# A decoder trunk on one Trainium2 core: two plain feature tiles instead of four ahead of the seven-product groups

## The chip, the core and the metric

The kernel runs on one NeuronCore of a Trainium2 chip. Its engines are TensorE (PE in the profile, its weight loads PEld), VectorE (DVE), ScalarE (ACT), GpSimd (POOL) and SyncE (SP); each takes its own instructions in order and waits for others by semaphores. The metric is the device time of one execution in microseconds (us), and the time given is the median over runs.

## What is computed

One step of a two-layer decoder trunk in float32, for 512 prompt tokens and 8 sample tokens at once (520 columns). Layer 0 mixes by a short convolution, layer 1 by sliding-window attention; both then have a feed-forward part and a gated embedding. The change lies in the feed-forward part:

```python
hf = rmsnorm(h, norm_ffn_g[i])
h = h + (jax.nn.silu(hf @ ffn_w_gate[i]) * (hf @ ffn_w_up[i])) @ ffn_w_down[i]
```

D_MODEL is 1024 and FFN_HIDDEN 2816, so gate and up have 22 feature tiles of 128 each.

## The kernel before

Activations lie feature-major: 128 partitions of features by 520 tokens, eight such tiles for the model width. Float32 products are made of three passes of a rounded type: each operand is split into a high half (a cast on ScalarE) and a low half (source minus high half, on VectorE, or by ScalarE and an accumulating transfer on POOL's queue, `low` with `dma`), and high by high, high by low and low by high are summed in PSUM.

In `ffn` the 22 feature tiles of gate and up are made in two ways. The first NP = 4 tiles are plain: `dense` runs 8 x 3 x 2 = 48 matmuls of 260 columns for each of the eight tensors (gate and up of four tiles), on the operands `fx` that need no norm factor; `nf.start` and `nf.spread` run among the first two and give the factor r. Lines 549 to 553 scale, apply silu and multiply. The other 18 tiles are made in ND = 9 groups of two tiles of gate and up. `gate_up` makes such a group as a 2 by 2 block product with seven products instead of eight, in the order 1, 6, 5, 7, 2, 3, 4. A product is 24 matmuls, so a group has 168 where the plain way has 192. The seven products need:

- seven activation operands, once a layer: the generator `operands` scales h to xn1 (tag D3) and xn2 (tag DP), forms t1 to t4 (E2 to E5) and splits everything to xs 1 to 7 (D4 to D10). The low halves of xs 2, 3 and 4 come by transfer.
- seven weight operands, once a group: the generator `weights` loads four blocks a11, a12, a21, a22 (w0r to w3r in the profile, 512 KB each), splits a11 for product 1, forms s1 = a21 - a22 (line 469) and s2 = s1 - a11 (line 470) for products 5 and 6, s3 = a21 - a11 (line 475) and s4 = a12 + s2 (line 480) for 7 and 3. s1 and s3 lie in tag D3, s2 and s4 in DP, so they take over the memory of xn1 and xn2. The low halves of a12 and a22 (wlE, tags E4 and E5, after t3 and t4) come by transfer; all other halves go through a ring of five buffers, the loads through a ring of six.

Each step of a generator ends at a `yield`; `prod` calls `next(ahead)` ahead of each product, so weights run two steps ahead. The text's order gives the priority: the program's scheduler fixes each engine's order by it among the instructions that it takes to be ready, and places the waits.

In the kernel before, the seven steps of `operands` are spread over the plain tensors by the tuple of line 554, and the first two weight steps stand ahead of the last plain tensor (lines 541 to 543). The results of all tiles lie in `hid`; the down projection splits them in that order and runs behind the last group.

Of the kernel before, what the change touches and what calls it, by code (L numbers as in the profile page):

```python
# [10 lines left out]
F32 = mybir.dt.float32  # L11
# [10 lines left out]
T = S + NB  # L22
TH = T // 2
KD = D // 128
FF = 2816
MF = FF // 128
NP = 4
ND = (MF - NP) // 2
PLE = 256
KP = PLE // 128  # L30
# [27 lines left out]
def _program(nc, a, o):  # L58
# [3 lines left out]
    with tile.TileContext(nc) as tc, ExitStack() as ctx:  # L62
        cp = ctx.enter_context(tc.tile_pool(name="const", bufs=1))
# [14 lines left out]
        def temp(name, dt=F32, shape=None):  # L78
            return tp.tile(shape or [128, T], dt, tag="t", name=name)
# [11 lines left out]
        def halves(t):  # L91
            return t.rearrange("p (a c) -> p a c", a=2)


        def slot(tag, shape, dt, name):
            return ap.tile(shape, dt, tag=tag, name=name)
# [5 lines left out]
        def preload(func, after):  # L102

            t = sp.tile([128, 1], F32, tag="pre", name=f"pre{func.name}")
            A.activation(t, after[:, :1], func, scale=0.0)
# [21 lines left out]
        def xpair(i, name):  # L127
            t = slot(f"X{i}", [128, 2, T], F32R, name)
            return t[:, 0, :], t[:, 1, :]
# [14 lines left out]
        def split_to(pair, src):  # L144
            A.copy(pair[0], src)
            V.tensor_tensor(pair[1], src, pair[0].bitcast(F32), ALU.subtract)
# [6 lines left out]
        def wsplit(w, name, step=8, dst=None):  # L153

            kt = w.shape[1]
            res = []
            for k0 in range(0, kt, step):
                n = min(step, kt - k0)
                raw = wr.tile([128, 8, 128], F32, tag="raw", name=f"{name}r{k0}")
                nc.sync.dma_start(raw[:, :n], w[:, k0:k0 + n, :])  # L160
                for q0 in range(0, n, 4):
                    q = min(4, n - q0)
                    if dst is None:
                        pr = wp.tile([128, 2, 4, 128], F32R, tag="pair", name=f"{name}p{k0 + q0}")
                    else:
                        pr = dst[:, :, k0 + q0:k0 + q0 + q]
                    A.copy(pr[:, 0, :q], raw[:, q0:q0 + q])
                    V.tensor_tensor(pr[:, 1, :q], raw[:, q0:q0 + q], pr[:, 0, :q].bitcast(F32), ALU.subtract)
                    res += [(pr[:, 0, i, :], pr[:, 1, i, :]) for i in range(q)]
            return res  # L170
# [8 lines left out]
        def dense(w, xs, name, mid=None, ws=None):  # L179
            ps = ps2(name)  # L180
            ws = ws or wsplit(w, name)
            for k in range(len(ws)):
                if mid and k in mid:
                    mid[k]()
                dense_k(ps, ws, xs, k)
            return ps[:, :, :TH]
# [161 lines left out]
        for j in range(KD):  # L348
            pc = pc1 if j == 1 else dense(a["w_in"][3 * j], cx, f"pc{j}") if j else None
            px_ = dense(a["w_in"][3 * j + 1], cx, f"px{j}") if j else None  # L350
            if j == 0:
                r = nm.r
                r2 = cp.tile([128, T], F32, tag="r2", name="r2")
# [25 lines left out]
        def operands(i, nf):  # L379

            n = f"{i}"
            x1 = slot("D3", [128, 4, T], F32, f"xn1{n}")
            x2 = slot("DP", [128, 4, T], F32, f"xn2{n}")
            for k in range(KD):
                V.scalar_tensor_tensor((x1, x2)[k // 4][:, k % 4], h[k], gain((N_FFN0, N_FFN1)[i], k), nf.r,
                                       ALU.mult, ALU.mult)
                if k % 4 == 3:
                    yield  # L390
            b11, b12, b21, b22 = x1[:, :, :TH], x1[:, :, TH:], x2[:, :, :TH], x2[:, :, TH:]
            t1, t2, t3, t4 = (slot(f"E{q}", [128, 4, TH], F32, f"t{q}{n}") for q in range(2, 6))
            res = {}

            def split(p, src, tag, dma=False):
                t = slot(tag, [128, 2, 4, TH], F32R, f"xs{p}{n}")
                A.copy(t[:, 0], src)
                low(t[:, 1], src, t[:, 0], dma)
                res[p] = t

            split(1, b11, "D4")
            V.tensor_tensor(t1, b12, b11, ALU.subtract)
            V.scalar_tensor_tensor(t2, t1, -1.0, b22, ALU.mult, ALU.subtract)
            yield
            split(6, t2, "D5")
            split(5, t1, "D6")
            yield
            V.tensor_tensor(t3, b12, b22, ALU.add)
            V.tensor_tensor(t4, t2, b21, ALU.add)
            yield  # L410
            split(2, b21, "D8", True)
            split(3, b22, "D9", True)
            yield
            split(7, t3, "D7")
            split(4, t4, "D10", True)
            yield res
# [114 lines left out]
        def ffn(i, fx, nf):  # L531

            hid, w = [], {}
            ops = operands(i, nf)
            ahead = weights(i, w)
            plain = [(a[f"w_{n}"][i, m], f"{n[0]}{i}{m}") for m in range(NP) for n in ("gate", "up")]
            mid = [{MID: nf.start}, {4: nf.spread}]
            ws, ps, xs = wsplit(*plain[0]), [], None
            for j in range(2 * NP):
                wn = wsplit(*plain[j + 1]) if j + 1 < 2 * NP else None  # L540
                if wn is None:
                    for _ in range(2):
                        next(ahead)
                ps.append(dense(None, fx, plain[j][1], mid[j] if j < 2 else None, ws))
                ws = wn
                if j % 2:
                    m = j // 2
                    t, u = temp(f"tg{i}{m}"), temp(f"tu{i}{m}")
                    V.tensor_tensor(halves(t), ps[j - 1], halves(nf.r), ALU.mult)
                    A.activation(t, t, AF.Silu)  # L550
                    V.tensor_tensor(halves(u), ps[j], halves(nf.r), ALU.mult)
                    hid.append(cp.tile([128, T], F32, tag=("tabc", "tabs", "k32", "r2")[m], name=f"hid{i}{m}"))
                    V.tensor_tensor(hid[m], t, u, ALU.mult)
                for _ in range((0, 2, 1, 1, 2, 1, 0, 0)[j]):
                    xs = next(ops)
            for d in range(ND):
                if d < KD:
                    t = slot(f"X{d}", [128, 2, T], F32, f"hid{i}d{d}")
                    out = [t[:, 0], t[:, 1]]
                else:  # L560
                    out = [cp.tile([128, T], F32, tag=tag, name=f"hid{i}{tag}") for tag in ("acc", "r")]
                gate_up(i, d, xs, w, ahead, out)
                hid += out
            hid2, ws = [], []
            for j, tag in enumerate(("D3", "E0", "E1", "E2", "D4", "D5", "D6", "D7", "D8", "D9", "D10", "E3", "E4", "E5")):
                if j % 5 == 0:
                    ws += wsplit(a["w_down"][i, 0, :, j // 5 * 8:min(j // 5 * 8 + 8, MF)], f"d{i}0{j}")
                nw = 1 if tag[0] == "E" else 2
                t = slot(tag, [128, nw, 2, T], F32R, f"hid{i}{tag}")
                for q in range(nw):  # L570
                    hid2.append((t[:, q, 0, :], t[:, q, 1, :]))
                    split_to(hid2[-1], hid[len(hid2) - 1])
            hid = hid2
            dp = slot("DP", [128, KP, 2, T], F32R, f"p{i}")
            pe = [(dp[:, q, 0, :], dp[:, q, 1, :]) for q in range(KP)]
            px = [xpair(k, f"px{i}{k}") for k in range(KD)]
            nq = Norm(f"q{i}")
            for m in range(KD):
                if m == 2:
                    preload(AF.Sigmoid, h[0])  # L580
                    for q in range(KP):
                        pt = temp(f"pt{i}{q}")
                        nc.sync.dma_start(pt, a["pT"][i, :, q, :])
                        split_to(pe[q], pt)
                pd = dense(a["w_down"][i, m], hid, f"d{i}{m}", ws=ws if m == 0 else None)
                resid(m, pd, nq, ((N_PLE0, N_PLE1)[i],), (px,))
            return px, pe, nq
# [12 lines left out]
        for i in range(KD + 1):  # L600
# [4 lines left out]
            m = i - 1  # L605
# [11 lines left out]
        tabc = const("tabc", [128, T])  # L617
        tabs = const("tabs", [128, T])
# [33 lines left out]
        r = nk.r  # L652
# [416 lines left out]
def _layout(i):  # L1069
# [7 lines left out]
    g, u = _wtiles(i["ffn_w_gate"]), _wtiles(i["ffn_w_up"])  # L1077
    r["w_gate"], r["w_up"] = g[:, :NP], u[:, :NP]
    gu = np.stack([g[:, NP:], u[:, NP:]], 3).reshape(2, ND, 2, 128, 2, 2, 4, 128)
    r["w_gu"] = gu.transpose(0, 1, 2, 5, 3, 4, 6, 7).reshape(2, ND, 4, 128, 2, 4, 128)  # L1080
# [43 lines left out]
```

## Time and profile before

| | us |
|---|---|
| median of 3 runs | 1235.63 |
| lowest, highest | 1235.51, 1235.92 |
| the profiled execution's own time | 1234.81 |
| its span | 1233.0 |
| TensorE busy in the span | 1211.8 |
| VectorE busy in the span | 828.3 |
| ScalarE busy in the span | 599.1 |

The span runs from the first to the last instruction on the core; 1.8 us of the execution's own time lie around it. Times in the rows below are counted from the span's start. Matmul ends are modelled, so a row's duration holds some overlap with the next; starts are exact.

### The profile page before, as it was taken

What the parts mean: (1) busy time and instruction counts of PE and PEld (TensorE: products, weight loads), DVE (VectorE), ACT (ScalarE), POOL (GpSimd) and SP (SyncE); (2) the same over time, 40 slices, a digit from 0 to 9 for tenths busy, and PEclk for the clock granted to TensorE, in tenths of its full rate; (3) what the DMA queues carried; (4) which work ended last, traced back from release to release, by engine and by line L of the source; (5) the groups of instructions that cost most, each with busy time, mean ns of one, the idle gap of its engine ahead of it and who ended that gap; (6) DMA issues with size and microseconds to landing.
All of it is one profiled execution on the core that took longest, in us unless ns stands there. A gap on an engine that the chain in (4) does not pass through costs nothing.

```text
span 1233.0 us, 23972 instructions
## 1 busy us (share of the span) xinstructions
PE 1211.8 (98%) x9901; PEld 1196.0 (97%) x9901; DVE 828.3 (67%) x1443; ACT 599.1 (49%) x1044; POOL 96.1 (8%) x135
## 2 busy tenths in 40 slices
PE   9999999999999999999998999999999999999996
PEld 8999999999999999999998979999999999999996
DVE  6845557786868843338888777787686877333565
ACT  6322344555555732334554787654555566323431
POOL 2000000101010000000033321000101010000000
PEclk9999999999999999999999999999999999999998
DMA  6222333856565433322541131346656552332312
GB/s 216 87 90 99 89 90 118 206 154 152 157 154 138 99 112 95 94 74 86 153 122 53 36 94 52 112 121 186 151 159 154 155 133 65 112 94 83 129 40 70
DMA packets 55133, 141.30 MB, mean 115 GB/s; under 512 B 5488, under 2 KB 20848, under 8 KB 55024
## 3 DMA queue, kind: packets, MB, share of 16 engines
q1 hardware_dynamic: 47296, 117.66, 30.7%
q0 software_dynamic: 7584, 22.07, 9.7%
q8 instruction: 78, 1.28, 0.4%
q14 instruction: 31, 0.25, 0.1%
q10 hardware_dynamic: 144, 0.03, 0.0%
HBM read 113.10 MB, written 4.58 MB: 95 GB/s over the span
## 4 chain that ended last, share of the span: by engine, by line
PE 90%; DVE 6%; ACT 1%; POOL 1%; DMA 1%; issue 1%; SPq 0%; DVEq 0%; POOLq 0%; ACTq 0%
PE d L176 20%; PE pb L490 13%; PE pd L490 9%; PE pa L490 8%; PE o L176 4%; PE po L176 4%; PE pg L176 4%; PE g L176 4%; PE u L176 4%; PE pc L176 3%; PE pb L176 3%; PE px L176 3%; PE pg L201 3%; PE av L770 1%; PE q L176 1%; PE pt L757 1%
## 5 line engine op out<-in xcount | busy, mean ns | idle before, releaser
L490 PE MATMUL pb<-xs,wh 128*128 128x260 f32 x864 | 158.9, 283 | 0.0
L490 PEld LDWEIGHTS pb<-xs,wh 128*128 128x128 f32 x864 | 133.4, 188 | 0.0
L446 ACT CAST wh<-s 128x1024 fp32r<-128x1024 f32 x72 | 75.6, 1051 | 75.1 <-PE pd L490 55.7
L424 DVE TENSOR_TENSOR wl<-s,wh 128x1024 fp32r<-128x1024 f32 x72 | 88.0, 1222 | 32.4 <-PE pb L490 26.7
L490 PE MATMUL pd<-xs,wh 128*128 128x260 f32 x576 | 106.9, 286 | 0.0
L490 PE MATMUL pa<-xs,wh 128*128 128x260 f32 x576 | 105.3, 283 | 0.0
L490 PEld LDWEIGHTS pd<-xs,wh 128*128 128x128 f32 x576 | 88.6, 188 | 1.4
L490 PEld LDWEIGHTS pa<-xs,wh 128*128 128x128 f32 x576 | 88.8, 188 | 0.0
L490 PE MATMUL pb<-xs,wl 128*128 128x260 f32 x288 | 81.5, 283 | 0.0
L490 PE MATMUL pd<-xs,wl 128*128 128x260 f32 x288 | 81.4, 282 | 0.0
L490 PEld LDWEIGHTS pd<-xs,wl 128*128 128x128 f32 x288 | 54.2, 188 | 0.0
L490 PEld LDWEIGHTS pb<-xs,wl 128*128 128x128 f32 x288 | 54.2, 188 | 0.0
L490 PE MATMUL pa<-xs,wlE 128*128 128x260 f32 x144 | 40.7, 283 | 0.0
L490 PE MATMUL pa<-xs,wl 128*128 128x260 f32 x144 | 40.7, 282 | 0.0
L490 PE MATMUL pb<-xs,wlE 128*128 128x260 f32 x144 | 40.6, 282 | 0.0
L504 DVE TENSOR_TENSOR u<-pd,u 128x520 f32<-128x520 f32 x36 | 25.0, 694 | 22.6 <-PE pd L490 22.6
L201 PE MATMUL pg<-px,wg 128*128 128x260 f32 x288 | 37.0, 283 | 0.0
L201 PEld LDWEIGHTS pg<-px,wg 128*128 128x128 f32 x288 | 35.5, 188 | 0.0
L422 POOL DMA_DIRECT2D wlE<-w1r x18 | 15.4, 856 | 223.1 <-ACT wlE L421 223.1
L446 ACT CAST wh<-w3r 128x1024 fp32r<-128x1024 f32 x18 | 18.9, 1052 | 26.9 <-PE pb L490 26.9
L736 ACT ACTIVATE P<-P,nmx 128x256 f32<-128x256 f32 (+1 forms) x64 | 30.2, 474 | 1.6 <-DVE nmx L728 1.1
L446 ACT CAST wh<-w1r 128x1024 fp32r<-128x1024 f32 x18 | 18.9, 1052 | 21.9 <-PE pb L490 21.9
(965 smaller groups left out, 3171.1 us busy)
## 6 DMA issues: line engine op xcount, KB each, us to landing
w1r<-in_w_gu SPq DMA_DIRECT2D x18, 512.0 KB, 3.6
w0r<-in_w_gu SPq DMA_DIRECT2D x18, 512.0 KB, 3.5
w2r<-in_w_gu SPq DMA_DIRECT2D x18, 512.0 KB, 3.5
wlE<-w1r POOLq DMA_DIRECT2D x18, 512.0 KB, 5.8
w3r<-in_w_gu SPq DMA_DIRECT2D x18, 512.0 KB, 3.7
wlE<-w3r POOLq DMA_DIRECT2D x18, 512.0 KB, 4.5
h<-in_xT SPq DMA_DIRECT2D x8, 260.0 KB, 5.9
xs<-xn POOLq DMA_DIRECT2D x4, 520.0 KB, 6.7
```

What stands on the lines that cost most here:

```text
L176: TE.matmul(ps[:, c, :TH], l, r[:, c * TH:(c + 1) * TH], start=(k == 0 and i == 0), stop=(k == len(ws) - 1 and i == 2))
L201: TE.matmul(ps, l, r[:, cols], start=(k == 0 and i == 0), stop=(k == n - 1 and i == 2))
L422: G.dma_start(out=dst, in_=src, accum_op=ALU.add)
L424: V.tensor_tensor(dst, src, hi.bitcast(F32), ALU.subtract)
L446: A.copy(hi, src)
L490: TE.matmul(ps[:, e, :TH], w[l][:, e, k, :], x[:, r, k, :], start=(start and k == 0 and q == 0), stop=(k == 3 and q == 2), skip_group_chec ...
L504: V.tensor_tensor(dst, ps, src, ALU.add)
L736: A.activation(P[:, j, :w], P[:, j, :w], AF.Exp, bias=nmx[:, j:j + 1], accum_out=sm[:, j:j + 1])
L757: TE.transpose(pt[:, j * 128:(j + 1) * 128], self.P[u][:, j, c * 128:(c + 1) * 128], ident)
L770: TE.matmul(po, self.vv[:, x, b, e * HD:e * HD + 128], PT[y][:, c], start=(e == 0 and c == 0 and i == 0), stop=(e == 1 and c == nk_ - 1 an ...
```

## The change

NP becomes 2 and ND, which follows from it, 10. The plain loop has four tensors instead of eight, and the seven operand steps are spread over them as 0, 2, 2, 3. The first two weight steps stand behind the whole plain loop, the last operand steps included. The tenth group needs a place for its outputs, so the ninth takes the tags k32 and r2, which plain tiles 2 and 3 had. The host packs the weights accordingly (`_layout` uses NP and ND).

```diff
-NP = 4
+NP = 2
 ND = (MF - NP) // 2
...
             for j in range(2 * NP):
                 wn = wsplit(*plain[j + 1]) if j + 1 < 2 * NP else None
-                if wn is None:
-                    for _ in range(2):
-                        next(ahead)
                 ps.append(dense(None, fx, plain[j][1], mid[j] if j < 2 else None, ws))
...
-                    hid.append(cp.tile([128, T], F32, tag=("tabc", "tabs", "k32", "r2")[m], name=f"hid{i}{m}"))
+                    hid.append(cp.tile([128, T], F32, tag=("tabc", "tabs")[m], name=f"hid{i}{m}"))
                     V.tensor_tensor(hid[m], t, u, ALU.mult)
-                for _ in range((0, 2, 1, 1, 2, 1, 0, 0)[j]):
+                for _ in range((0, 2, 2, 3)[j]):
                     xs = next(ops)
+            for _ in range(2):
+                next(ahead)
             for d in range(ND):
...
-                    out = [cp.tile([128, T], F32, tag=tag, name=f"hid{i}{tag}") for tag in ("acc", "r")]
+                    out = [cp.tile([128, T], F32, tag=tag, name=f"hid{i}{tag}") for tag in (("k32", "r2"), ("acc", "r"))[d - KD]]
                 gate_up(i, d, xs, w, ahead, out)
```

## Rows read from the trace of the kernel before

**Rows 1.** The page's first part: engines' busy time, share of the span, instructions.
```profile
PE 1211.8 (98%) x9901; PEld 1196.0 (97%) x9901; DVE 828.3 (67%) x1443; ACT 599.1 (49%) x1044; POOL 96.1 (8%) x135
```

**Rows 2.** The chain that ended last: start us, us, what; both gate and up stages.
```profile
218.39 5.76 PE g L176 x48
...
241.43 2.88 PE pa L490 x24
...
424.22 126.69 PE d L176 x1056
...
824.92 5.76 PE g L176 x48
...
847.96 2.88 PE pa L490 x24
...
1030.69 125.26 PE d L176 x1044
```

**Rows 3.** Busy us by stretch: PE, PEld, DVE, ACT, POOL, then clock, DMA share, GB/s.
```profile
205.00:218.00 13.00, 13.00 (x111) 13.00 (x110) 13.00 (x19) 9.22 (x12) 1.45 (x1) 1.00 0.30 66
218.00:241.27 23.27, 23.27 (x197) 23.27 (x195) 17.05 (x21) 11.77 (x16) 3.88 (x4) 1.00 0.84 200
...
302.40:322.60 20.20, 20.20 (x170) 20.10 (x169) 15.07 (x19) 10.97 (x14) 1.71 (x2) 1.00 0.60 155
```

**Rows 4.** VectorE in order: start us, us, line, operation, [idle before, releaser].
```profile
211.62 0.68 DVE L168 TENSOR_TENSOR u01p<-u01r,u01p 128x512 fp32r<-128x512 f32 x1
212.22 1.23 DVE L424 TENSOR_TENSOR xs<-xn,xs 128x1040 fp32r<-128x1040 f32 x1
213.37 1.23 DVE L402 TENSOR_TENSOR t<-xn 128x1040 f32<-128x1040 f32 x1
...
229.42 1.23 DVE L475 TENSOR_TENSOR s<-w2r,w0r 128x1024 f32<-128x1024 f32 x1 [0.66 <-DMA w2r<-in_w_gu]
...
237.51 1.22 DVE L469 TENSOR_TENSOR s<-w2r,w3r 128x1024 f32<-128x1024 f32 x1 [5.05 <-DMA w3r<-in_w_gu]
238.66 1.22 DVE L424 TENSOR_TENSOR wl<-w0r,wh 128x1024 fp32r<-128x1024 f32 x1
239.79 1.22 DVE L470 TENSOR_TENSOR s<-s,w0r 128x1024 f32<-128x1024 f32 x1
...
818.38 0.69 DVE L168 TENSOR_TENSOR u11p<-u11r,u11p 128x512 fp32r<-128x512 f32 x1
```

**Rows 5.** ScalarE in order, layer 0.
```profile
211.73 1.06 ACT L397 CAST xs<-xn 128x1040 fp32r<-128x1040 f32 x1 [1.28 <-DVE xn L387]
212.70 1.07 ACT L421 ACTIVATE xs<-xn 128x1040 fp32r<-128x1040 f32 x1
213.67 0.60 ACT L167 CAST g02p<-g02r 128x512 fp32r<-128x512 f32 x1
...
237.59 1.06 ACT L421 ACTIVATE wlE<-w3r 128x1024 fp32r<-128x1024 f32 x1 [3.71 <-DMA w3r<-in_w_gu]
...
241.12 1.05 ACT L446 CAST wh<-s 128x1024 fp32r<-128x1024 f32 x1 [1.29 <-DVE s L470]
```

**Rows 6.** POOL's first operand transfer; landing of all three in layer 0.
```profile
214.08 1.45 POOL L422 DMA_DIRECT2D xs<-xn  x1 [70.46 <-ACT xs L421]
...
DMA to landing us min/median/max: 5.2/6.1/7.1
```

**Rows 7.** TensorE's wait in the attention's first part, and the stretches behind it.
```profile
674.64 0.33 PE L757 MATMUL pt<-ident,P 128*128 128x128 f32 x1 [1.74 <-ACT P L745]
...
674.00:676.00 2.00, 1.36 (x8) 1.36 (x9) 0.80 (x2) 1.66 (x9) 1.05 (x2) 0.73 0.00 0
676.00:678.00 2.00, 2.00 (x10) 1.91 (x10) 1.89 (x10) 1.58 (x5) 0.00 (x0) 0.50 0.00 0
678.00:680.00 2.00, 2.00 (x15) 1.91 (x15) 1.14 (x5) 1.30 (x4) 1.26 (x2) 0.91 0.00 0
```

## Prediction

> **What bounds the kernel now.** I read the page's first part, then the chain of waits, then the two gate and up stages engine by engine. The first part shows TensorE busy for nearly the whole span and VectorE for two thirds of it [rows 1]. The chain of waits shows what the reader should see next: in the stage that the change touches the chain lies on TensorE without a break, from the plain tiles through the nine groups into the down projection [rows 2]. A plain tensor (48 matmuls) takes 5.76 us, one of the seven products (24 matmuls) 2.88 us. So TensorE sets the pace there, and fewer matmuls would be a gain if nothing else came late.
>
> The third view, busy time by stretch, says how near that is. Right after the norm factor arrives, VectorE is busy 13.00 of 13.00 us; in the next stretch, the last four plain tensors, 17.05 of 23.27; in a settled group 15.07 of 20.20 [rows 3]. The share of 67% over the span hides a stretch with no slack at all. VectorE's order of work [rows 4] shows what it does there: the seven activation operands, the plain tiles' own evictions and weight halves, and after them the first group's weight combinations. It falls idle for 5.05 us at the end of that, waiting for a load. That idle time, and the 23.04 us of the last four plain tensors, are the cover under which the groups' operands are made. The change takes away the 23.04 us.
>
> **What it removes from TensorE.** Per layer two plain feature tiles go (four tensors, 4 x 5.76 = 23.04 us) and one group comes. The nine groups of layer 0 take 424.22 - 241.43 = 182.79 us, 20.31 each; those of layer 1 take 1030.69 - 847.96 = 182.73, 20.30 each [rows 2]. The gain is 2.73 + 2.74 = **5.5 us**, all of it on the chain.
>
> **What comes earlier.** Without the two tiles TensorE reaches the first group at 218.39 us in layer 0 and 824.92 in layer 1, where a third plain tile begins now [rows 2]. Product 1 takes 2.88, so product 6 could start at 221.27 and 827.80. Product 6 needs the low half of its weights (wl of product 6, line 424), which VectorE makes from s2, which comes from s1.
>
> What must VectorE do before that? It takes work by program order among what is ready: the combination of line 475 ran at 229.42, ahead of the s1 of line 469, which waited for its load until 237.51 [rows 4]. In the changed program both weight steps stand behind all seven operand steps. So I count from the instruction at 211.62, which ends the part that both kernels share (818.38 in layer 1). Starts lie 0.60 us apart for a 512 or 520 wide instruction (211.62 to 212.22), 1.15 for 1040 (212.22 to 213.37) and 1.13 for 1024 (238.66 to 239.79) [rows 4]:
> - the second half of the last plain tensor's weights: 0.60
> - three evictions of plain tile 1 (lines 549, 551, 553): 3 x 0.60 = 1.80
> - operands: low halves of xs 1, 5, 6 and 7 and the sums t1 to t4: 8 x 1.15 = 9.20
> - weights: low half of product 1, s1, s2, s3 (it fits while ScalarE casts s2) and low half of product 6: 5 x 1.13 = 5.65, and 0.09 more as the last one counts in full (1.22)
>
> That is 17.34 us: it ends at 228.96 in layer 0 and 835.72 in layer 1. Product 6 comes 228.96 - 221.27 = 7.7 and 835.72 - 827.80 = 7.9 us late, together **15.6 us**. The weight loads are not what is late: line 469 waited because a raw buffer was held by a plain tensor, and four plain tensors fewer use those buffers.
>
> **What a wait of that length adds.** TensorE would stand still from 218.39 until product 1's low half is there (three instructions and the cast's fill before 228.96, some 224.4), then run one product. The trace has no wait of 6 us, so I bound its after-effect. Behind a wait of 1.74 us the granted clock is 0.73, 0.50 and 0.91 over three stretches of 2 us, that is the lower level (1.2 GHz) for 1.08 + 2.00 + 0.36 = 3.4 us [rows 7]; at half rate that loses 1.7 us. The loss is nothing if it falls on product 1, which at 224.4 + 2.88 + 1.7 = 229.0 would end just as product 6's weights arrive, and 1.7 if it falls behind product 6. I take the middle, 0.85 a layer, **1.7 us** in all, and keep 0 and 3.4 for the range.
>
> **What is moved and costs nothing by my reading.** The two moved weight steps issue four loads on SP's queue, two ScalarE multiplications with an accumulating transfer each on POOL's queue (a12 and a22), and two casts. On SP's queue four plain loads of the same size are gone ahead of them. On POOL's queue they stay behind the three operand transfers, as now. The a12 transfer follows t3, the a22 one t4's own transfer; with 5.2 to 7.1 us for a transfer [rows 6] they land by some 232 and 238, and products 2 and 4 begin at 228.96 + 3 x 2.88 = 237.6 and 243.4. If that cover were gone, each us late would be a us lost. Outputs of the ninth group go to k32 and r2, the tenth's to acc and r: free by then. The tenth group adds VectorE work at 15.07 in 20.20 us, which the settled groups carry without a wait of TensorE. The down projection starts behind a group as before.
>
> By the rule of the Trainium skill (Perfetto Trace Analysis, "Identifying the Most-Contended Engine") one improves the engine with the highest occupancy; by the page's first part that is TensorE, and the whole 5.5 us would be gained. The stretch of 13.00 in 13.00 on VectorE speaks against it here (the same page says that regimes can change), and it stands below as the first rival.
>
> **Sum.** 15.6 + 1.7 - 5.5 = +11.8 us. The profiled execution took 1234.81 us, so 1246.6 on its scale; the median of the runs is 0.82 higher, 1235.63, which gives **1247.4**.
>
> **Rivals.**
> - The cover is enough (faster). VectorE would have to finish product 6's low half by 221.27, 7.7 us sooner than counted; six or seven of the 1.15 us instructions would have to run before 211.62 or after product 6. For it: there are idle gaps on VectorE around the norm. Against it: the operands hang on the norm factor, and none of them can start before it. Time: 1235.63 - 5.5 = 1230.1. It decides at a delay of 2.7 us a layer. Chance 0.07.
> - The weights go ahead of t3, t4 and xs 7, and something else is last (slower, but less). s2 is written to the tile that shares its memory with xn2 (tag DP), and xn2 is read by the transfers of xs 2 and 3. ScalarE can first touch xn2's second half at 211.73 and needs four instructions of 0.97 us for the two (212.70 to 213.67), 215.6; POOL issues 0.3 later; 6.1 to 7.1 us on, the second transfer has landed at 222.0 to 223.0. Then s2, 1.33 us to its cast, some 1.15 for the cast, 1.22 for the low half: 225.7 to 226.7 [rows 4 to 6]. Delay 4.4 to 5.4 a layer, with 0 to 3.4 for the clock and 5.5 gained: +3.3 to +8.7, or 1239 to 1244. Chance 0.14. By the Trainium skill (DMA: Bandwidth & Descriptors, "Anatomy of one DMA") such a transfer would take 2.0 us and its bytes at 436 GB/s, an estimate of 3.2 us for 520 KB, and this floor would vanish; the trace has 5.2 to 7.1, and decides.
> - ScalarE is stuck ahead of product 6's cast (slower by more). The a22 multiplication writes to the slot of t4, so it waits for t4's transfer to xs 4. If it is queued ahead of the cast of s2, the cast waits behind it, as casts did at 237.59 behind a wait of 3.71 us for a load [rows 5]. t4 is ready at about 222, two ScalarE instructions and the issue bring 224.4, the transfer 229.6 to 231.5; the multiplication, cast and low half then end at 233 to 235, 4 to 6 us later than counted. In one layer 1251 to 1254, in both 1255 to 1260. Chance 0.19.
> - The two effects cancel: part of VectorE's order is favourable and the clock does not fall; within 2.5 us of before. Chance 0.05.
>
> **How the numbers follow.** The forecast keeps 0.55, with 1244 to 1250 of its own from the clock's two ends and s3 in or out of the count. The range of 8 in 10 goes from 1239 to 1256: it leaves out the first and the last rival and the top of the third. A difference under 0.2% (2.5 us) is about what a measurement of this kernel cannot tell from none. Faster 0.07, same 0.06, slower 0.87.
>
> **What would show it.** Right: in both stages TensorE idle ahead of the first group, released by VectorE's low halves (line 424), product 6 starting 6 to 9 us behind the last plain tensor's end plus 2.88, groups after that at 20.3 us, the granted clock dipping once a stage, and nothing else moved. Wrong: first-group products without a gap, or a gap released by a ScalarE multiplication of line 421 or a transfer of line 422. A second gap in the second group would mean that VectorE has not caught up.

## The result and the profile after

The changed kernel takes 1254.47 us (median; 1250.53 to 1256.85), the kernel before 1235.57 beside it (1235.02 to 1235.92). The ratio is 1.014, with a 95% interval of 1.0123 to 1.0157: slower by some 18 us. The profiled execution of after took 1256.85 us, its span 1255.0.

First the page's first part (after): busy us, share of the span, instructions.

```profile
PE 1217.4 (97%) x9853; PEld 1200.9 (96%) x9853; DVE 841.4 (67%) x1451; ACT 610.1 (49%) x1052; POOL 99.1 (8%) x139
```

TensorE has 48 matmuls less than in [rows 1] and is busy longer, which no count of instructions explains; VectorE still stands at 67%. Next the stretches (after): the gate and up stage of layer 0, the stretch from the k projection to layer 1's first plain tensor, the stage of layer 1. The last row is the middle stretch of before. Columns as in [rows 3].

```profile
192.62:432.79 240.17, 232.80 (x1895) 231.38 (x1893) 187.05 (x240) 136.64 (x182) 20.74 (x23) 0.98 0.60 149
618.09:811.61 193.52, 185.92 (x1399) 176.60 (x1397) 151.35 (x411) 124.50 (x319) 46.58 (x70) 0.96 0.27 84
811.61:1051.77 240.16, 231.88 (x1887) 230.21 (x1885) 186.82 (x240) 136.28 (x181) 20.61 (x23) 0.98 0.58 143
```
```profile
609.35:799.95 190.60, 183.34 (x1399) 173.76 (x1397) 151.20 (x411) 124.37 (x319) 46.58 (x70) 0.98 0.28 85
```

Before, the two stages took 230.93 us (193.13 to 424.06) and 230.58 (799.95 to 1030.53). So layer 0 lost 9.24 and layer 1 lost 9.58, **18.8 us** together, which is the difference of the medians (18.9). The middle stretch is 2.92 longer in this execution with the same matmuls in the same order and a lower mean clock, 0.96 for 0.98. Over all profiled executions below it lies between 187.4 and 195.0, so a single execution can be off by some us there, and I compare kernels by the length of the two stages.

Where in the stage? The chain of waits (after), layer 0 from VectorE's last steps to the down projection, then layer 1:

```profile
222.84 1.15 DVE wl L424
...
224.03 5.15 PE pa L490 x22
...
229.18 1.04 ACT wh L446
...
230.25 1.24 DVE wl L424
...
231.53 4.14 PE pb L490 x22
...
250.15 2.88 PE pa L490 x24
...
432.95 126.69 PE d L176 x1056
...
842.36 4.67 DMA xs<-t
...
850.40 4.44 PE pb L490 x22
...
869.16 2.88 PE pa L490 x24
...
1051.93 125.26 PE d L176 x1044
```

In [rows 2] this chain never leaves TensorE. Now it runs through VectorE, ScalarE and, in layer 1, a transfer. The last nine groups take 432.95 - 250.15 = 182.80 us, 20.31 each, exactly as before. All of the loss lies in the first group: TensorE has done the last plain tensor at 217.89 (218.39 of [rows 2] less 0.50, by which everything here runs earlier) and begins the second group at 250.15, 32.26 us instead of 20.31. TensorE's waits (after; us in total, times, longest):

```profile
PE pa L490 <- DVE wl L424: 12.0, 2, 6.1
...
PE pb L490 <- ACT wh L446: 1.9, 2, 1.2
...
PE pb L490 <- DVE wl L424: 1.5, 2, 0.8
```

A long wait ahead of product 1, for its low half, and two short ones ahead of product 6: for ScalarE's cast and for VectorE's low half. VectorE, then ScalarE in order (after, layer 0), two rows of layer 1 behind:

```profile
211.12 0.69 DVE L168 TENSOR_TENSOR u01p<-u01r,u01p 128x512 fp32r<-128x512 f32 x1
...
225.03 1.22 DVE L475 TENSOR_TENSOR s<-w2r,w0r 128x1024 f32<-128x1024 f32 x1
226.17 1.22 DVE L470 TENSOR_TENSOR s<-s,w0r 128x1024 f32<-128x1024 f32 x1
...
230.25 2.36 DVE L424 TENSOR_TENSOR wl<-s,wh 128x1024 fp32r<-128x1024 f32 x2 [1.60 <-ACT wh L446]
...
843.48 1.23 DVE L469 TENSOR_TENSOR s<-w2r,w3r 128x1024 f32<-128x1024 f32 x1 [0.58 <-DMA w2r<-in_w_gu]
```
```profile
225.14 1.05 ACT L446 CAST wh<-s 128x1024 fp32r<-128x1024 f32 x1 [1.06 <-DVE s L469]
228.22 1.06 ACT L421 ACTIVATE wlE<-w3r 128x1024 fp32r<-128x1024 f32 x1 [2.03 <-DMA xs<-t]
229.18 1.03 ACT L446 CAST wh<-s 128x1024 fp32r<-128x1024 f32 x1
...
847.09 1.06 ACT L421 ACTIVATE wlE<-w3r 128x1024 fp32r<-128x1024 f32 x1 [1.31 <-DMA xs<-t]
```

VectorE works without a break from 211.12 to 228.65, as counted. Then it is idle for 1.60, which the count had not: the cast of s2, whose operand was ready at 227.39, stands on ScalarE behind the a22 multiplication (line 421), and that waits for the transfer of xs 4. The same in layer 1 at 847.09. And the granted clock, in the column ahead of the DMA share (after):

```profile
224.00:226.00 2.00, 1.97 (x9) 1.97 (x10) 2.00 (x2) 0.94 (x2) 1.17 (x2) 0.50 0.68 132
...
230.00:232.00 2.00, 0.98 (x6) 0.77 (x7) 1.75 (x2) 1.65 (x3) 0.42 (x1) 1.00 0.98 203
232.00:234.00 2.00, 2.00 (x15) 2.00 (x14) 0.60 (x1) 0.00 (x0) 0.00 (x0) 0.69 1.06 373
234.00:236.00 2.00, 2.00 (x11) 2.00 (x11) 0.45 (x1) 0.30 (x1) 0.00 (x0) 0.50 1.04 213
```

It falls twice in the stage: behind the long wait, onto product 1 (5.15 us for 22 matmuls), and again behind the two short waits, onto product 6 (4.14).

### The profile page after: what moved, and what is told of

It is laid out like the page before. It is cut to its first block, busy times and chain, and to the rows that moved or that the text cites. A ratio compares the mean times of both kernels' runs of the same rounds, so it can differ in the third digit from the quotient of the medians.

```text
span 1255.0 us, 23907 instructions
## 1 busy us (share of the span) xinstructions
PE 1217.4 (97%) x9853; PEld 1200.9 (96%) x9853; DVE 841.4 (67%) x1451; ACT 610.1 (49%) x1052; POOL 99.1 (8%) x139
## 4 chain that ended last, share of the span: by engine, by line
PE 86%; DVE 9%; ACT 2%; issue 1%; DMA 1%; POOL 1%; DVEq 0%; POOLq 0%; ACTq 0%
PE d L176 20%; PE pb L490 14%; PE pd L490 9%; PE pa L490 9%; PE o L176 4%; PE po L176 4%; PE pg L176 4%; PE pc L176 3%; PE pb L176 3%; PE px L176 3%; PE pg L201 3%; PE q L176 1%; PE av L769 1%; PE pt L756 1%; PE pj L176 1%
## 5 line engine op out<-in xcount | busy, mean ns | idle before, releaser
L490 PE MATMUL pb<-xs,wh 128*128 128x260 f32 x960 | 179.4, 285 | 1.9 <-ACT wh L446 1.9
L490 PEld LDWEIGHTS pb<-xs,wh 128*128 128x128 f32 x960 | 150.4, 191 | 2.3 <-ACT wh L446 2.3
L424 DVE TENSOR_TENSOR wl<-s,wh 128x1024 fp32r<-128x1024 f32 x80 | 97.7, 1223 | 42.9 <-PE pb L490 34.0
L490 PE MATMUL pa<-xs,wh 128*128 128x260 f32 x640 | 120.5, 288 | 0.0
L490 PE MATMUL pd<-xs,wh 128*128 128x260 f32 x640 | 119.3, 286 | 0.0
L490 PEld LDWEIGHTS pa<-xs,wh 128*128 128x128 f32 x640 | 101.8, 194 | 0.0
L490 PEld LDWEIGHTS pd<-xs,wh 128*128 128x128 f32 x640 | 99.0, 189 | 1.6
L490 PE MATMUL pb<-xs,wl 128*128 128x260 f32 x320 | 92.1, 288 | 1.5 <-DVE wl L424 1.5
L490 PE MATMUL pd<-xs,wl 128*128 128x260 f32 x320 | 90.6, 283 | 0.0
L490 PEld LDWEIGHTS pa<-xs,wl 128*128 128x128 f32 x160 | 32.1, 201 | 12.5 <-DVE wl L424 12.5
```

Source lines behind the costliest of these rows:

```text
L424: V.tensor_tensor(dst, src, hi.bitcast(F32), ALU.subtract)
L490: TE.matmul(ps[:, e, :TH], w[l][:, e, k, :], x[:, r, k, :], start=(start and k == 0 and q == 0), stop=(k == 3 and q == 2), skip_group_chec ...
```

## The experiments

Each kernel was timed beside the kernel before on the same chip, whose median there was 1235.25 to 1236.51 us. The table has the median, its ratio to that kernel with the interval, the start of product 6's low half (line 424) counted from the first plain matmul of its stage, and the length of the two stages from that matmul to the first of the down projection. By the prediction the low half would have begun at 34.61 and 34.55 (its end, 228.96 and 835.72, less 1.22 and less the stage's start).

| kernel | us | ratio | low half of 6, layer 0 / 1 | stage, layer 0 / 1 |
|---|---|---|---|---|
| before | 1235.57 | 1 | not waited for | 230.93 / 230.58 |
| after | 1254.47 | 1.014 (1.0123 to 1.0157) | 37.63 / 37.51 | 240.17 / 240.16 |
| e1, six plain tiles | 1238.38 | 1.0016 (1.0006 to 1.0025) | not waited for | 233.68 / 233.70 |
| e4, steps moved alone | 1237.28 | 1.0004 (0.9993 to 1.0014) | not waited for | 230.94 / 230.64 |
| e2, a22 behind the cast | 1248.64 | 1.0099 (1.0079 to 1.0119) | 35.93 / 36.71 | 237.00 / 237.84 |
| e3, filler | 1256.21 | 1.0158 (1.0143 to 1.0174) | 37.62 / 37.53 | 241.68 / 241.42 |
| e13, filler, longer | 1251.39 | 1.0141 (1.0124 to 1.0158) | 37.62 / 37.53 | 239.13 / 239.11 |
| e9, VectorE work added | 1258.31 | 1.0181 (1.0163 to 1.0198) | 38.38 / 38.32 | 241.98 / 240.70 |
| e6, sums on GpSimd | 1259.08 | 1.0186 (1.0169 to 1.0204) | 38.17 / 39.85 | 241.64 / 242.58 |
| e7, e6 and filler | 1259.18 | 1.0182 (1.0157 to 1.0206) | 38.18 / 39.70 | 241.11 / 243.29 |
| e12, sums left out | 1255.99 | 1.0171 (1.0156 to 1.0186) | 37.59 / 37.37 | 239.83 / 240.12 |
| e14, e12 and filler | 1256.60 | 1.0178 (1.0163 to 1.0194) | 37.26 / 38.70 | 240.26 / 241.51 |
| e10, product 5 first | 1256.78 | 1.0173 (1.0149 to 1.0198) | other order | 239.07 / 243.04 |
| e17, product 6 served first | 1252.65 | 1.0149 (1.0131 to 1.0168) | 31.17 / 38.87 | 236.74 / 242.32 |

**What a group saves.** The kernel before, with one group fewer instead of one more:

```diff
-NP = 4
+NP = 6
```

> Six plain tiles and eight groups, the two weight steps ahead of the last plain tensor as before. Tests the term of the gain. If TensorE sets the pace wherever the operands are covered, a group less and two plain tiles more cost 23.04 - 20.31 = 2.73 us a layer, 5.5 us in all: 1241.1 us, with no new wait of TensorE in either stage. If instead the groups or the down projection carry a hidden wait that a group less would take away, less than 3 us.

The stages grew by 2.75 and 3.12 us, the 2.73 and 2.74 of the prediction and 0.4 more in layer 1, with no new wait. The time missed what I expected: it is 1.9 us above the kernel before, not 5.5. In its one profile the middle stretch is shorter (187.37 us), and the 1.5 us wait for q3b, a tile of the attention, that before and after carry in it is missing there. So the term of the gain is shown by the stages, not by the time.

**Does the move itself cost?** The kernel before, with the two weight steps behind the plain loop, as the change has them, but four plain tiles:

```diff
-                if wn is None:
-                    for _ in range(2):
-                        next(ahead)
...
+            for _ in range(2):
+                next(ahead)
```

> The kernel before with four plain tiles, and only the first two weight steps moved behind the plain loop. Tests the move alone. With four plain tiles VectorE has 5 us idle ahead of the first group, so by the count of its work the low half of product 6 would be ready within about 3 us of TensorE's arrival at worst: 0 to 3 us a layer, 1235.6 to 1242. If the place of the two steps is what costs, not the missing tiles, most of the 9.4 us a layer that the changed kernel lost would be here too: 1250.

Nothing: 0.01 and 0.06 us of stage, no new wait. While the 23.04 us of cover are there, the move costs nothing. Whether its place matters once the cover is gone, this run cannot say: no run has two plain tiles with only the two weight steps back in their old place. e17 below, which among other things takes the weights of products 1 and 6 further ahead, suggests for layer 0 that it does.

**Is it VectorE or ScalarE?** The change, with the a22 multiplication of the first group held behind the cast of s2:

```diff
                 split(d, 6, s2)
+                if d == 0:
+                    wle(a22, "E5", res[d, 6][0])
```

Here `wle` makes the copy, the multiplication and the transfer; in the old place it is called for a22 from the second group on.

> The changed kernel, with one edit: in the first group of each layer the ScalarE multiplication of a22 is made to follow the cast of s2 (a copy of one column block of that cast into its slot comes first). Tests whether ScalarE's queue sets product 6. In the changed kernel the multiplication waits for t4's transfer and ends at 229.18, the cast of s2 then at 230.22, the low half at 231.48; s2 itself is ready at 227.4. If the queue sets it, the cast moves to 227.5 and the low half to some 229.9, 1.6 us a layer sooner, and product 6 starts close behind product 1, so that the second fall of the clock goes too, 1.7 us a layer: 3.2 to 6.6 us less than the changed kernel, about 1248 to 1251. If VectorE's count alone sets it, no change: 1254.

1248.64, inside what the first theory expected; the stages are 3.17 and 2.32 us shorter than in the change. ScalarE, VectorE, the chain and the clock of layer 0, and last TensorE's waits and the chain at product 6 in layer 1:

```profile
227.88 1.05 ACT L446 CAST wh<-s 128x1024 fp32r<-128x1024 f32 x1 [1.27 <-DVE s L476]
```
```profile
228.97 2.35 DVE L424 TENSOR_TENSOR wl<-s,wh 128x1024 fp32r<-128x1024 f32 x2
```
```profile
224.44 5.13 PE pa L498 x22
229.57 0.43 PE pd L498 x2
230.01 3.14 PE pb L498 x24
```
```profile
228.00:230.00 2.00, 2.00 (x12) 2.00 (x10) 2.00 (x2) 1.32 (x2) 0.00 (x0) 0.53 1.11 195
230.00:232.00 2.00, 2.00 (x17) 1.80 (x16) 1.32 (x2) 1.97 (x4) 0.21 (x1) 1.00 1.03 219
```
```profile
PE pb L498 <- ACT wh L446: 0.9, 1, 0.9
PE pb L498 <- DVE wl L424: 0.8, 1, 0.8
...
844.61 2.93 PE pb L498 x22
```

The cast now waits for s2 itself, and the low half comes 2.40 us behind the start of s2, where the change had 230.25 - 226.17 = 4.08 in layer 0 and 849.12 - 845.75 = 3.37 in layer 1. So ScalarE's queue cost 1.68 and 0.97. The rest of the gain is the clock: product 6 runs at 1.00 in both layers (22 matmuls in 2.93 us in layer 1, for 4.44 in the change). In layer 0 the two short waits ahead of it are gone. In layer 1 they are not, 0.9 and 0.8 us are left, and the clock does not fall. So the second fall disappears when the cast is no longer held up, but short waits of this length do not bring it by themselves, and what does stays open. What remains, 6.07 and 7.26 us of stage more than before, hangs on VectorE (the waits of 5.9 and 6.1 ahead of product 1), with 0.73 us of waiting for a load (w2r) in layer 1.

**Does VectorE's count set that remainder?** e2 with four useless 520 wide subtractions ahead of s1:

```diff
+            for q in range(4):
+                V.tensor_tensor(halves(temp(f"x{q}{n}")), res[7][:, 1, 0:2].bitcast(F32), res[7][:, 0, 0:2].bitcast(F32), ALU.subtract)
```

> e2_a22_after_cast with four useless 520 wide subtractions (4 x 0.60 = 2.4 us a layer) on VectorE between product 1's low half and s1; nothing of the result uses them. Theory (VectorE's count sets product 6): its low half comes 2.4 us later, 231.4; product 1 starts as in e2 and ends at 229.6, so TensorE waits about 1.8 us there, 1.8 to 2.4 a layer on the chain: 1252 to 1253.5, and up to 1.7 a layer more if this second wait brings a second fall of the clock, 1257 at most. Rival (a transfer or ScalarE sets it): unchanged, 1248.6.

The added work took 2.44 us and moved the low half by 2.45 in layer 0:

```profile
224.64 2.53 DVE L417 TENSOR_TENSOR x<-xs 128x520 f32<-128x520 f32 x4
227.08 1.22 DVE L477 TENSOR_TENSOR s<-w2r,w3r 128x1024 f32<-128x1024 f32 x1
```

VectorE's count sets product 6, one for one. In layer 1 it moved by 1.61, since the 0.73 us of waiting for w2r went under it. The time was above the top of what I expected (1257): the stage of layer 0 grew by 4.98, for behind the waits of 1.76 and 0.52 that the delay opened the clock fell onto product 6, as in the change.

The opposite, VectorE relieved of t3 and t4, with e2 below it:

```diff
-            V.tensor_tensor(t3, b12, b22, ALU.add)
-            V.tensor_tensor(t4, t2, b21, ALU.add)
+            G.tensor_tensor(t3, b12, b22, ALU.add)
+            G.tensor_tensor(t4, t2, b21, ALU.add)
```

> As e2_a22_after_cast (the a22 multiplication behind the cast of s2), and the two sums t3 and t4 are made by GpSimd instead of VectorE; the same is computed. VectorE's row ahead of product 6's low half is two instructions of 1.15 us shorter, and product 1's low half comes ahead of most of it. Theory (VectorE's count sets product 6): product 1 starts without a wait at about 217.9, the low half of product 6 at about 226.7 instead of 228.97, so the single wait, about 5.9 us, moves from ahead of product 1 to ahead of product 6. What the time makes of it depends on the clock. If the half clock that followed the 5.9 us wait in e2 (about 6 us of it, 3 us of work) now falls on product 6 and 5, most of the 2 x 2.9 us is lost again: 1245 to 1249. If waits have no after-effect of this kind: 1242 to 1243.5. Rival (ScalarE or a transfer sets product 6, VectorE does not): low half of product 6 still at 228.9 or later, 1248.6 or more.

A miss: product 6's low half came 2.24 and 3.14 us later than in e2, not 2.3 earlier. VectorE, then POOL:

```profile
215.67 2.89 DVE L403 SCALAR_TENSOR_TENSOR t<-t,xn 128x1040 f32<-128x1040 f32 x1
...
219.62 5.27 DVE L424 TENSOR_TENSOR xs<-t,xs 128x1040 fp32r<-128x1040 f32 x2
```
```profile
212.42 5.04 POOL L408 TENSOR_TENSOR t<-xn,xn 128x1040 f32<-128x1040 f32 x1 [68.26 <-DVE xn L387]
...
219.13 3.50 POOL L409 TENSOR_TENSOR t<-t,xn 128x1040 f32<-128x1040 f32 x1
```

VectorE's t2 takes 2.89 us instead of 1.23 and the pair of xs 5 and 6 takes 5.27 instead of 2.39 while GpSimd's sums run: 4.54 lost for 2.3 saved. The run doesn't take VectorE's load away, it adds to it, and the time follows, as VectorE's count would have it. It is no test of the relief. Two further runs stand on this kernel:

> e6_two_sums_on_gpsimd with 50 useless matmuls (128x128 on the identity, 0.114 us each by the run e3_busy_while_waiting, 5.7 us in all) between product 1 and product 6 of the first group of each layer; nothing of the result uses them. If the clock's after-effect is a real price on the chain: product 6 and 5 run at full clock, 2 to 3 us a layer less than e6, 1241.5 to 1244. If the filler ends early and a rest of the wait stays, the clock falls behind that and it is like e6. If the clock costs nothing on the chain: same as e6, or later by as much as the filler outlasts the wait.

> The change mended as far as the rows allow: t3 and t4 on GpSimd, and in the first group of each layer the order of products 1, 5, 6, 2, 7, 4, 3 instead of 1, 6, 5, 7, 2, with the weight step of s1 (which product 5 needs) ahead of the operand of product 7; the same is computed. Theory: VectorE has the low half of product 5 at about 222.5 to 223.5 (due 220.8), s2 waits for the xs 2 and xs 3 transfers until 222 to 223, the low half of product 6 comes at 226 to 227.5 (due 226.1 by then), product 2 waits for the a12 transfer until about 231 (due 230). Lateness 3.5 to 5 a layer, less 2.73, and 0 to 1.7 for the clock: 1237 to 1243, better than the change and not better than the kernel before. Rival (the whole 5.5 us can be had by a better order): under 1234.

e7 (e6 with `keep_busy(f"{i}b", 50)` ahead of product 6) is as slow as e6: the wait had grown by what GpSimd cost, and 3.60 us of it remained behind the filler. e10 (e6 with product 5 ahead of product 6 in the first group) is 1256.78, a miss of the 1237 to 1243 expected: product 5's low half began at 34.65 behind the stage's start, late for the same reason. Neither tells more.

The relief without GpSimd: e2 without the two sums.

```diff
-            V.tensor_tensor(t3, b12, b22, ALU.add)
-            V.tensor_tensor(t4, t2, b21, ALU.add)
...
-            split(7, t3, "D7")
-            split(4, t4, "D10", True)
+            split(7, t1, "D7")
+            split(4, t2, "D10", True)
```

> e2_a22_after_cast without the two sums t3 and t4 (t1 and t2 stand in for them, so products 7 and 4 get other operands): two VectorE instructions of 1.15 us less a layer, and none on GpSimd. Theory (VectorE's count sets product 6): product 1's low half comes early, product 1 starts at about 217.9 without a long wait, and product 6's low half is ready at about 227.5 instead of 230.2; the one wait of 6 to 7 us then lies between product 1 and product 6. By the runs e6 and e9, where such a wait lay there, the clock after it was half for about 6 us, 3 us of work lost on the chain where e2 lost none: 1248 to 1251, so hardly a gain for 2.7 us a layer less of VectorE work. Without a price of the clock: 1243 to 1244. Rival (VectorE doesn't set it): low half of product 6 not before 230.

> e12_sums_left_out with 60 useless matmuls (0.114 us each, 6.8 us) between product 1 and product 6 of the first group of each layer, so that TensorE works through the wait. If the half clock after a wait is a price on the chain: the clock stays at 1.00 and e14 is 4 to 7 us faster than e12, 1243 to 1246. If not: the same as e12 within 1.5 us.

Both missed, by my own edit. s2 began 2.29 us earlier than in e2 (31.24 behind the stage's start, for 33.53), but ScalarE stood still (e12, layer 0; ScalarE, then VectorE):

```profile
229.03 1.99 ACT L444 CAST wh<-s 128x1024 fp32r<-128x1024 f32 x2 [6.80 <-DMA xs<-t]
```
```profile
231.06 2.36 DVE L422 TENSOR_TENSOR wl<-s,wh 128x1024 fp32r<-128x1024 f32 x2 [3.88 <-ACT wh L444]
```

With t2 as the source of xs 4, its tile (E3), which is also the fifth weight buffer, is read by xs 4's transfer, and the casts wait for that. It says nothing on VectorE's share, but it is the same mechanism as a22's: an instruction in ScalarE's order waits for a slot that a transfer still reads, and the cast that TensorE needs stands behind it.

**What does the clock cost?** The change with useless matmuls on the identity ahead of product 1 (n0) and of product 6 (n1) of the first group, e3 with 48 and 24, e13 with 54 and 43:

```diff
+            keep_busy(f"{i}a", n0)
             for d in range(ND):
...
+            if d == 0:
+                keep_busy(f"{i}b", n1)
             prod(pb, 6, True)
```

> The changed kernel with matmuls of no use (identity by identity, 128 columns) in TensorE's waits: 48 ahead of product 1 and 24 ahead of product 6 of the first group of each layer, some 5.3 and 2.6 us by the 0.11 us of such a matmul in the attention. Nothing else moves. Tests the price of the clock. The trace of the changed kernel has the granted clock at half twice in each stage, for the whole of product 1 and for most of product 6. Product 1 at half rate ends ahead of product 6's weights, so its loss is hidden; product 6's is not. If so, full clock gives back 1.7 us a layer, 3.4 us: about 1251, and the times of the runs lie closer together. If the clock costs nothing because the wait covers it, 1254; if both falls cost, 1246.

A miss: product 1 ran at full clock, but a rest of the second wait stayed open, and the clock fell behind it (e3; TensorE, then a stretch):

```profile
230.98 0.51 PE L490 MATMUL pb<-xs,wh 128*128 128x260 f32 x2 [0.68 <-ACT wh L446]
232.24 0.59 PE L490 MATMUL pb<-xs,wl 128*128 128x260 f32 x1 [0.75 <-DVE wl L424]
```
```profile
234.00:236.00 2.00, 2.00 (x11) 2.00 (x11) 0.00 (x0) 0.00 (x0) 0.00 (x0) 0.50 1.10 256
```

> The change, with 54 useless matmuls ahead of product 1 and 43 ahead of product 6 of the first group of each layer: like e3_busy_while_waiting, where 48 and 24 left rests of 0.55, 0.68 and 0.75 us and the clock fell on product 6, but long enough to leave no rest. Clock theory: product 6's low part starts at about 232.4 at full clock, 3.4 us a layer less than e3 and about 1.7 a layer less than the change itself: 1250 to 1252. If the clock's fall has no price on the chain: 1254 to 1256.

With the filler over the whole of both waits no wait is left, and the clock is 1.00 for all of layer 0's stage (e13; a stretch, then the chain):

```profile
193.69:432.82 239.13, 239.13 (x1991) 238.27 (x1990) 186.83 (x240) 136.66 (x181) 20.74 (x23) 1.00 0.59 150
```
```profile
228.00 4.75 PE busy0b L497 x43
232.75 2.92 PE pb L490 x24
```

The stages are 1.04 and 1.05 us shorter than in the change, though product 6 starts 0.39 us later on the stage's scale (232.75 less 1.07, against 231.53 less the 0.24 of its first two matmuls). So the fall costs the change 1.4 us in layer 0, and 1.5 in layer 1 by the same working (product 6 starts 0.47 us later there). The medians alone (1251.39 and 1254.47, intervals that overlap) would not have shown it.

**Can the order be mended?** The change with s1 and s2 in one tile (D3) and s3 and s4 in the other (DP), the weights of products 1 and 6 ahead of the operands of 5 and 7 and of tu and hid, and the a12 and a22 multiplications of the first group behind the cast of s1 (the diff is cut to the main lines):

```diff
-                s13 = slot("D3", [128, 2, 2, 4, 128], F32, f"s13{n}")
-                s24 = slot("DP", [128, 2, 2, 4, 128], F32, f"s24{n}")
+                s12 = slot("D3", [128, 2, 2, 4, 128], F32, f"s12{n}")
...
+                s34 = slot("DP", [128, 2, 2, 4, 128], F32, f"s34{n}")
...
+                        for g in (ahead, ahead, ops, ahead, ops):
+                            next(g)
```

> The change with the order of VectorE's work mended, and the same computed: s1 and s2 share one tile (D3) and s3 and s4 the other (DP), so that s2 no longer waits for the readers of xn2; product 1's low half, s1, s2 and product 6's low half stand ahead of the operands of products 5 and 7 and of the evictions of tu and hid; the a12 and a22 multiplications come behind the cast of s1. By VectorE's count the low half of product 6 is ready at about 225 instead of 231.5 in the change and 230.2 in e2. Due 220.3 to 220.5: 4.6 late a layer, up to 3.4 more for product 7's low half and product 2's transfer, less 2.73 gained, and 0 to 1.7 for the clock: 1239.5 to 1246. If VectorE's order is not what sets the first group: 1248 or more. If the whole gain can be had: under 1234.

In layer 0 the low half began at 31.17, 6.46 us sooner than in the change, and the stage is 3.43 shorter; of the rest 1.4 us are further waits of TensorE in that group (0.50, 0.44 and 0.44 us). In layer 1 two other limits took its place (e17; VectorE, then ScalarE):

```profile
839.50 1.23 DVE L471 TENSOR_TENSOR s<-w2r,w3r 128x1024 f32<-128x1024 f32 x1 [1.23 <-DMA w2r<-in_w_gu]
```
```profile
842.84 1.06 ACT L420 ACTIVATE wlE<-w3r 128x1024 fp32r<-128x1024 f32 x1 [4.03 <-DMA xs<-t]
```

There s1 waits for a load that is issued late, and a22 stands ahead of the cast again; TensorE waits 9.5 us in one piece. Hence 1252.65 instead of 1239.5 to 1246. None of these versions beats the kernel before; whether an order exists that pays stays open.

## Why the prediction was right, and where it was not

The sign, the place and the chief mechanism are as predicted, and 1254.47 lies in the range; the forecast, 1247.4, is 7.1 us too low, and the time lies outside the 1244 to 1250 that the forecast allowed itself. That it lies in the range is in part luck. The top, 1256, is 1.5 us above it. The range left out the top of the rival in which ScalarE is held up in both layers (1255 to 1260). That case came, and it stayed cheaper because xs 4's transfer landed early and s2, which the cast needs, was late by an error of the count.

The signs that the prediction set were met in part. TensorE was idle ahead of the first group and released by line 424, and later groups take 20.3 us. But product 6's first matmul started 9.5 and 9.7 us behind the last plain tensor's end plus 2.88, not 6 to 9; the clock dipped twice; and a sign of being wrong showed too, for one short gap ahead of product 6 comes from the multiplication of line 421, and in layer 1 the chain runs through a transfer of line 422. Step by step:

- **The gain, 5.5 us.** Right: later groups at 20.31 us, and e1 shows the term from the other side.
- **VectorE's count.** Right in kind: no break in VectorE's work, TensorE released by line 424, e9 moves product 6 one for one, and e17 moves it the other way in layer 0. No run took work off VectorE without another limit taking its place (e6, e12). e4 shows that the move costs nothing while the cover is there. The size was off. By the count the low half begins at 34.6 behind the stage's start; in e2, where a22 is out of its way, it begins at 35.93 and 36.71. The step "s3 (it fits while ScalarE casts s2)" failed: VectorE did s3 (225.03) ahead of s2 (226.17) and s4 under the cast, so one 1.13 us instruction more stood ahead. Why the scheduler took s3 first no run shows. In layer 1 a wait of 0.58 us for w2r came on top; the sentence that the weight loads are not what is late was wrong by that much.
- **ScalarE behind a22**, given 0.19 as a rival, came in both layers, beside the forecast rather than instead of it: 1.68 and 0.97 us, not the 4 to 6 it was priced at. xs 4's transfer had landed by 228.2, not between 229.6 and 231.5, and part of the wait fell beside s2, which was itself late.
- **The clock.** The half level came behind the long wait as expected and was hidden there, as the lower bound said. What was missed is a second fall, onto product 6, behind two short waits (0.71 and 0.76 us in layer 0, 1.16 and 0.76 in layer 1). It costs 1.4 and 1.5 us (e13) instead of 0.85 a layer, inside the bounds of 0 and 1.7. It went when a22 was held back (e2), though in layer 1 with short waits left; so what brings it is not shown. "The granted clock dipping once a stage" was wrong.
- **The sum.** Forecast +11.8 for the two stages, measured +18.8. Of the 7.0, a22 is 2.7, w2r 0.6, the clock 1.2 (2.9 for 1.7), and s3 ahead of s2 about 2.7: that is what is left of the lateness of the low half (1.34 and 1.41), of which the instruction itself is 1.13 a layer. The terms come to 7.2, so they are known to some tenths.
- **The other rivals.** The cover was not enough by far. Transfers of xs 2 and 3 ended last nowhere, as the weights stood behind t3, t4 and xs 7. By the Trainium skill (Perfetto Trace Analysis, "Identifying the Most-Contended Engine") the busiest engine is the one to relieve. Here relieving it bought 5.5 us and cost 24.3, because in the first group VectorE was the bound; the measurement decides.
- **Costed at nothing.** The tenth group's VectorE work: right (nine groups at 20.31, no gap in the second group). Among what moved with the two weight steps, the a22 multiplication and, in layer 1, the load of w2r were costed at nothing too, and those two were not free, as said above; the move alone is, while the cover is there (e4).

## What to carry to other kernels

Before taking work off the busiest engine, ask what that work covers: count, from the stretch itself, what the other engines must finish before the next thing starts, and read the slack there, not in the share of the span. Then follow each queue that the cover had made harmless: here a multiplication that waited 2.03 and 1.31 us for a transfer to release its tile held back the cast that TensorE needed, and a second fall of the clock cost 1.4 to 1.5 us a layer on top. A stage's length, first matmul to first matmul, shows 1 us where medians do not.

## What the runs showed of the hardware

- GpSimd's sum of two 1040 wide operands took 5.04 and 3.50 us, and VectorE's instructions beside it 2.89 instead of 1.23 and 5.27 instead of 2.39 (e6). The Trainium skill (SBUF — State Buffer, "Who interferes with whom") says that a VectorE instruction with two inputs in SBUF contends with a GpSimd one that reads SBUF, and that the one that comes second waits. The trace agrees for the instructions named: the 2.89 us one began at 215.67, inside GpSimd's first sum (212.42 to 217.46), and ended at 218.56. Two others inside the same sum, at 212.76 and 213.91, kept their 1.24 us.
- Working through most of a wait did not keep the clock: with rests of 0.68 and 0.75 us behind a filler it still fell to 0.50 (e3), with no rest it stayed at 1.00 (e13). But waits of 0.92 and 0.76 us did not bring it down in layer 1 of e2, so the length of such a wait does not decide alone.
- The stretch between the stages varied from 187.4 to 195.0 us between profiled executions; before and after have the same matmuls in the same order there.
